# Both down-projections of a macaron decoder layer as seven half-size block products

## The chip, the cores and the metric

One core of a Trainium2 chip runs the whole layer as one program. The metric is the time of one execution on the device in microseconds (us), as the median of several runs. Engines that matter here: TensorE (PE) multiplies, VectorE (DVE) and ScalarE (ACT) prepare operands and take results away, GpSimd (POOL) does some element-wise work, and the queue of SyncE (SP) issues most transfers between DRAM and on-chip memory.

## What is computed

The layer has two feed-forward blocks, one at its start and one at its end, with attention between them. D = 1024 features, 1024 tokens, D_FF = 2816 hidden features:

```python
def swiglu(h, w1, w3, w2):
    return (jax.nn.silu(h @ w1) * (h @ w3)) @ w2

x = x + 0.5 * swiglu(rms_norm(x, norm_ffn1[l]), ffn1_w1[l], ffn1_w3[l], ffn1_w2[l])
...
x = x + 0.5 * swiglu(rms_norm(x, norm_ffn2[l]), ffn2_w1[l], ffn2_w3[l], ffn2_w2[l])
x = rms_norm(x, norm_out[l])
```

The change is in `(...) @ w2`, the product of the gated hidden values (called g here, 2816 x 1024 tokens) with w2 (2816 x 1024), and in how it is added to x.

## The kernel before

Everything is kept transposed: features on the 128 partitions, tokens along a row. A value of 32 bits is multiplied as two parts: `hi`, the rounded value in the type fp32r, and `lo`, what rounding took away. `split` (lines 162 and 163) makes them, `hi` by a copy on ACT and `lo` by a subtraction on DVE, or on POOL where a caller says so. `mm3` (lines 169 to 171) then does three matmuls, hi*hi, hi*lo and lo*hi, each 128 x 128 weights against up to 512 token columns.

**Up-projections.** `up` runs over eleven pairs c of 128-row hidden blocks (22 in all). For all pairs but the first, `strassen` already uses seven products in place of eight. The gated result of pair c, 128 x 2 x 1024 (j = 0, 1 are the two hidden blocks of the pair, then the tokens), is multiplied on POOL (line 493) and written to a DRAM tensor `ga`c in the first feed-forward and `gb`c in the second (line 494).

**Down-projections.** `down` goes through rounds, one for each half of the tokens h and half of the features fh (the second feed-forward takes its second half of the tokens as two pieces of 256 columns, all features at once). In a round it goes over the eleven pairs; each gives two k-blocks for four accumulators of 128 x 512 (PSUM tiles `mm` and `big`): 2 x 4 x 3 matmuls. The weights of the pair come by `unit` as one transfer of 512 KB into a `raw` tile (4 of them) on SP's queue, and are split into `w` and `v` tiles, `lo` on POOL in two of three cases. The g parts are read once per half of the tokens on ACT's queue (`load_g`, line 499) and kept in `a` tiles (33 in all) for both halves of the features. At a round's end DVE adds half of the accumulators to x (line 578). The rounds together are the plain eight block products of a 2 x 2 x 2 split, done at 1056 matmuls of 512 columns for the first feed-forward, and 528 of 512 and 1056 of 256 for the second.

**Order.** The program is written as one stream; a scheduler at build time moves instructions within it by priority and gives out tiles, and each engine then runs its own list strictly in order. Transfers wait in the issuing engine's list as any instruction does. `norm_x` (the next normalisation's scaling and squares) is stepped from inside the loop over `down`, and so are the output's statistics (`final_squares`, `final_stats`, `final_out`) in the second feed-forward.

Of the kernel before, what the change touches and what calls it, by code (L numbers as in the profile page):

```python
# [47 lines left out]
class Layer:  # L48
# [191 lines left out]
    def norm_x(self, gain, rt=None):  # L240


        self.r = self.a([P, 2, H])
        self.xn = [[], []]
        for h in range(2):
            acc = None
            for kp in range(4):
                x = self.x[h][kp]
                self.xn[h] += self.scaled(x, gain + 2 * kp)
                acc = self.squares([x], acc)  # L250
                if kp == 3:
                    self.late[h] = (acc, self.folded(acc), self.r[:, h], None if rt is None else rt[:, 4 * h:4 * h + 4])
                yield
# [216 lines left out]
    def up(self, base, name, ws, forms, beside=None):  # L470
# [4 lines left out]
        for c in range(1, NF // 2):  # L475
# [5 lines left out]
            for w in wv:  # L481
                for i, _ in enumerate(self.strassen(w)):
                    if c == NF // 2 - 1 and w is wv[1]:
                        if i == 1:
                            ready = [self.load_g(gd[n], 0) for n in range(2)]
                        if i == 5:
                            src = self.gated(gd, 0, ready)
                            self.g0 = src, [next(src)]
                outs.append(self.prod)
# [5 lines left out]
        return gd  # L495

    def load_g(self, d, h):
        raw = self.a([P, 2, H])
        self.nc.scalar.dma_start(out=raw, in_=d[:, :, h * H:h * H + H])
        return raw  # L500

    def gated(self, gd, h, ready=()):

        for c, d in enumerate(gd):
            raw = ready[c] if c < len(ready) else self.load_g(d, h)
            hi, lo = self.a([P, 2, H], F32R), self.a([P, 2, H], F32R)
            self.split(raw, hi, lo)
            yield hi, lo

    def down(self, base, gd, load, pieces=((0, 0, H), (1, 0, H))):  # L510
# [3 lines left out]
        g = {0: self.g0}  # L514

        def unit(c, fh, engine):
            raw = self.wr.tile([P, 2, H], F32, name="raw", tag="raw")
            u = base + U_W2A + 2 * c
            nc.sync.dma_start(out=raw, in_=self.wts[u:u + 2, :, fh * H:fh * H + H].rearrange("u p c -> p u c"))
            hi, lo = self.w([P, 2, H], F32R), self.v([P, 2, H], F32R)  # L520
            self.split(raw, hi, lo, engine)
            return hi, lo

        rounds = [(h, t0, t1, fh) for h, t0, t1 in pieces for fh in ((0, 1) if t1 - t0 == H else (None,))]
        for n, (h, t0, t1, fh) in enumerate(rounds):
            W = t1 - t0
            if fh is None:
                feats = list(range(8))
                ps = [self.big_ps([P, 2, 2, W]) for _ in range(2)] if n % 2 else [self.mm_ps([P, 2, W]) for _ in range(4)]
                ps = [p.rearrange("p a b t -> p (a b) t") for p in ps] if n % 2 else ps  # L530
                per = 4 if n % 2 else 2
            else:
                feats = list(range(4 * fh, 4 * fh + 4))
                ps = [self.big_ps() for _ in range(2)] if n % 2 else [self.mm_ps([P, 1, H]) for _ in range(4)]
                per = 2 if n % 2 else 1
            if n == 1:
                ahead = []
                g[1] = self.gated(gd, 1), ahead
            for kp in range(feats[0] // 2, feats[-1] // 2 + 1):
                if len(self.x[h]) <= kp:  # L540
                    self.x[h].append(load(h, kp))
            src, parts = g[h]
            for c in range(NF // 2):
                if len(parts) <= c:
                    parts.append(next(src))
                ws = []
                if fh is None:
                    ws += [self.weight(base + U_W2A + 2 * c + i, self.v if i else self.w, nc.vector if i else nc.gpsimd) for i in range(2)]
                else:
                    hi, lo = unit(c, fh, nc.vector if c % 3 == 2 else nc.gpsimd)  # L550
                    ws = [(hi[:, i], lo[:, i]) for i in range(2)]

                def one(i, f):
                    d = f - feats[0]
                    w = [v[:, d * P:d * P + P] for v in ws[i]]
                    self.mm3(ps[d // per][:, d % per], w, [v[:, i, t0:t1] for v in parts[c]],
                             c == 0 and i == 0 and d % per % 2 == 0 if W < H else c == 0 and i == 0,
                             c == NF // 2 - 1 and i == 1, W < H)

                if c == NF // 2 - 1:  # L560
                    for f in feats:
                        for i in range(2):
                            one(i, f)
# [649 lines left out]
    def run(self):  # L1213
# [14 lines left out]
        for step in self.down(0, gd, self.from_input):  # L1228
            if step is None:
                n += 1  # L1230
                if n in (2, 4, 6, 8, 9, 10):
                    next(norm)
# [130 lines left out]
```

## Time and profile before

| | |
|---|---|
| median of 3 runs | 2237.0 us (2234.97 to 2237.11) |
| the profiled execution | 2238.7 us, of which the span from first to last instruction is 2236.9 us |
| PE busy | 2187.7 us, 98% of the span |
| DVE / ACT / POOL busy | 56% / 44% / 26% |
| PE busy on the chain that ended last | 88% |
| data moved | 237.87 MB, 106 GB/s over the span |

The span falls into 40 slices on the page. The first down-projection lies between 494 and 737 us, the second between 1968 and 2223 us. Matmuls overlap in the records (each is shown for about twice its step), so what PE needs is read from the distance between two starts, not from the duration shown.

### The profile page before, as it was taken

How to read it: one execution, taken by the hardware profiler on the slowest of the kernel's cores; microseconds unless marked ns; L12 is line 12 of the kernel's file. 1: busy time of each engine (PE TensorE's matmuls, PEld its weight loads, DVE VectorE, ACT ScalarE, POOL GpSimd, SP SyncE). 2: the span in 40 equal slices, each digit the busy share in tenths (PEclk: the TensorE clock that was granted, in tenths of full speed). 3: DMA queues.
4: the chain of work that ended last, by engine and by line, in shares of the span. 5: the costliest groups of instructions: out<-in, count | busy, mean ns of one | idle time of the engine just before them, and what ended most of it. 6: DMA issues, size and time to landing. Idle time of an engine off the chain costs nothing.

```text
span 2236.9 us, 27311 instructions
## 1 busy us (share of the span) xinstructions
PE 2187.7 (98%) x10962; PEld 1849.2 (83%) x10962; DVE 1258.1 (56%) x1588; ACT 979.2 (44%) x1387; POOL 592.5 (26%) x363
## 2 busy tenths in 40 slices
PE   8999999999999999999999999999999999999997
PEld 7788888878888888878987788777888888878997
DVE  7964545443214677776556666867754545433433
ACT  6634333343323567654434354534433333433542
POOL 0033434353332000110011111100143434442353
PEclk9999999999999999999999999999999999999999
DMA  7322222256643211011123221222222222365654
GB/s 262 106 97 84 79 82 85 81 164 212 208 145 103 76 39 48 28 39 39 48 95 114 99 81 59 93 85 75 76 83 79 84 84 76 108 222 191 210 183 132
DMA packets 84639, 237.87 MB, mean 106 GB/s; under 512 B 7712, under 2 KB 10912, under 8 KB 84512
## 3 DMA queue, kind: packets, MB, share of 16 engines
q1 hardware_dynamic: 57328, 157.99, 22.2%
q0 software_dynamic: 15216, 55.06, 6.3%
q10 hardware_dynamic: 11968, 23.07, 3.2%
q8 instruction: 86, 1.41, 0.3%
q14 instruction: 41, 0.34, 0.0%
HBM read 191.00 MB, written 45.09 MB: 106 GB/s over the span
## 4 chain that ended last, share of the span: by engine, by line
PE 88%; DVE 6%; ACT 3%; issue 1%; DMA 1%; POOL 0%; SPq 0%; DVEq 0%; ACTq 0%; POOLq 0%
PE mm L170 17%; PE mm L169 17%; PE mm L171 17%; PE big L169 11%; PE big L170 11%; PE big L171 11%; PE big L896 1%; PE mm L942 1%; DVE a L163 1%; PE mm L218 1%; DMA raw<-in_wts_dram 1%; DVE w L163 1%; ACT t L147 1%; ACT w L162 1%; DVE v L163 0%
## 5 line engine op out<-in xcount | busy, mean ns | idle before, releaser
L169 PE MATMUL mm<-a,w 128*128 128x512 f32 (+1 forms) x1536 | 588.2, 383 | 5.6 <-ACT w L162 5.5
L170 PE MATMUL mm<-a,w 128*128 128x512 f32 (+1 forms) x1536 | 585.5, 381 | 5.0 <-DVE a L163 5.0
L162 ACT CAST w<-raw 128x1024 fp32r<-128x1024 f32 (+1 forms) x315 | 310.5, 993 | 503.4 <-PE mm L170 213.5
L163 POOL TENSOR_TENSOR v<-raw,w 128x1024 fp32r<-128x1024 f32 x120 | 290.3, 2419 | 621.2 <-ACT w L162 617.2
L171 PE MATMUL mm<-a,v 128*128 128x512 f32 (+1 forms) x1056 | 401.6, 380 | 0.0
L169 PE MATMUL big<-a,w 128*128 128x512 f32 (+1 forms) x1024 | 391.8, 383 | 5.3 <-DVE a L789 4.3
L170 PE MATMUL big<-a,w 128*128 128x512 f32 (+1 forms) x1024 | 390.2, 381 | 0.9 <-DVE a L163 0.8
L169 PEld LDWEIGHTS mm<-a,w 128*128 128x128 f32 x1536 | 291.8, 190 | 60.4 <-ACT w L162 5.5
L170 PEld LDWEIGHTS mm<-a,w 128*128 128x128 f32 x1536 | 291.7, 190 | 60.0 <-DVE a L163 7.2
L171 PE MATMUL big<-a,v 128*128 128x512 f32 (+1 forms) x800 | 302.9, 379 | 0.0
L171 PE MATMUL mm<-a,w 128*128 128x512 f32 (+1 forms) x632 | 233.4, 369 | 0.5 <-DVE w L163 0.5
L171 PEld LDWEIGHTS mm<-a,v 128*128 128x128 f32 x1056 | 198.6, 188 | 37.6
L169 PEld LDWEIGHTS big<-a,w 128*128 128x128 f32 x1024 | 193.0, 188 | 43.2 <-ACT a L783 4.5
L170 PEld LDWEIGHTS big<-a,w 128*128 128x128 f32 x1024 | 193.0, 188 | 37.8 <-DVE a L163 1.7
L163 DVE TENSOR_TENSOR a<-a 128x1024 fp32r<-128x1024 f32 (+2 forms) x105 | 126.0, 1210 | 160.1 <-ACT a L162 159.9
L417 DVE TENSOR_TENSOR a<-a,mm 128x1024 f32<-128x1024 f32 x40 | 48.9, 1221 | 258.6 <-PE mm L171 258.6
L171 PEld LDWEIGHTS big<-a,v 128*128 128x128 f32 x800 | 151.0, 189 | 28.6 <-issue 0.7
L163 DVE TENSOR_TENSOR w<-raw,w 128x1024 fp32r<-128x1024 f32 (+1 forms) x107 | 150.0, 1404 | 35.9 <-PE big L170 20.3
L162 ACT CAST a<-a 128x1024 fp32r<-128x1024 f32 (+2 forms) x105 | 98.2, 945 | 154.2 <-DMA a<-gb 61.0
L171 PE MATMUL big<-a,w 128*128 128x512 f32 (+1 forms) x440 | 162.6, 370 | 0.0
L171 PEld LDWEIGHTS mm<-a,w 128*128 128x128 f32 x632 | 121.7, 193 | 20.2 <-DVE w L163 1.0
L163 DVE TENSOR_TENSOR v<-raw,w 128x1024 fp32r<-128x1024 f32 x66 | 83.7, 1271 | 59.5 <-ACT w L162 59.2
(208 smaller groups left out, 3173.5 us busy)
## 6 DMA issues: line engine op xcount, KB each, us to landing
raw<-in_wts_dram SPq DMA_DIRECT2D x265, 512.0 KB, 3.7
ga<-a POOLq DMA_DIRECT2D x22, 512.0 KB, 2.9
a<-ga ACTq DMA_DIRECT2D x22, 512.0 KB, 4.4
gb<-a POOLq DMA_DIRECT2D x22, 512.0 KB, 2.9
a<-gb ACTq DMA_DIRECT2D x22, 512.0 KB, 4.6
a<-in_x_dram SPq DMA_DIRECT2D x16, 512.0 KB, 6.2
xm<-a POOLq DMA_DIRECT2D x8, 512.0 KB, 5.2
a<-xm POOLq DMA_DIRECT2D x8, 512.0 KB, 10.0
```

Of the source, the lines that this page charges most:

```text
L147: ins = self.nc.scalar.activation(out, in_, func, **kw)
L162: copy = self.nc.scalar.copy(hi, full)
L163: (engine or self.nc.vector).tensor_tensor(lo, full, hi.bitcast(F32), op=ALU.subtract)
L169: mm(ps, w[0], x[0], start=start, stop=False, skip_group_check=more)
L170: mm(ps, w[0], x[1], start=False, stop=False, skip_group_check=more)
L171: mm(ps, w[1], x[0], start=False, stop=stop, skip_group_check=more)
L218: self.nc.tensor.matmul(ps, self.ones_r if m is None else m, v, start=i == 0, stop=i == len(parts) - 1)
L417: nc.vector.tensor_tensor(out[1], c, b1.unsqueeze(1).broadcast_to([P, 2, H]), op=ALU.add)
L896: nc.tensor.matmul(ps[:, c, :n], qs[m][:, i, iq], xs[c][:, m, :n], start=i == 0, stop=i == 1)
L942: nc.tensor.matmul(op[:, ib % 4 * P:ib % 4 * P + P], v[jb // 4][:, jb % 4, par], at[:, jb * P:jb * P + P], start=jb == 0, stop=jb == ib)
```

## The change

The token halves h, the feature halves fh and the two blocks j of each pair make g and w2 into 2 x 2 blocks: G(j,h) with 1408 rows in eleven blocks of 128, W(j,fh) likewise. `down` now takes Strassen's scheme in Winograd's form: seven products, in the order 1, 5, 6, 3, 7, 4, 2, each over all eleven hidden blocks (five steps of two blocks and a last one of one) with four accumulators of 128 x 512. The operands are sums and differences of blocks, made on DVE (`less`, line 521 of the new file) from blocks that are read again for each product:

- product 1: G(0,0) with W(0,0); product 2: G(1,0) with W(1,0); product 3: G(1,1) with a sum of four W blocks; product 4: a sum of four G blocks with W(1,1); products 5, 6, 7: sums of two or three blocks on both sides.
- Products 6 and 7 go on in the accumulators of product 1, and product 3 in those of product 5. The accumulators are added to x after each product, to one quarter of x, after product 7 to two.
- g and w2 are read as transfers of 256 KB, two for a `raw` tile, all on SP's queue. Both splits are on ACT and DVE; POOL has no splits there any more. Running sums are kept in six `a` tiles (g) and six `v` tiles (weights). The g operands are made six steps ahead of PE, the weights' two.
- In the second feed-forward only product 2 is taken in two pieces of 256 columns. `final_squares` takes the other two feature pairs first, and the second half of the tokens is finished first.
- `norm_x` runs over the second half of the tokens first, and the first `diff_proj` after it does both of its projections for that half before the other.

```diff
-    def norm_x(self, gain, rt=None):
+    def norm_x(self, gain, rt=None, order=tuple((h, kp) for h in range(2) for kp in range(4))):
...
+        for h, kp in order:
+            x = self.x[h][kp]
+            self.xn[h][2 * kp:2 * kp + 2] = self.scaled(x, gain + 2 * kp)
...
                 for i, _ in enumerate(self.strassen(w)):
-                    if c == NF // 2 - 1 and w is wv[1]:
-                        if i == 1:
-                            ready = [self.load_g(gd[n], 0) for n in range(2)]
-                        if i == 5:
-                            src = self.gated(gd, 0, ready)
-                            self.g0 = src, [next(src)]
+                    if i == 1 and w is wv[1] and c == NF // 2 - 1:
+                        down = self.down(base, gd, load, pieces)
+                        with self.tc.high_priority(60):
+                            next(down)
...
+        order = (1, 5, 6, 3, 7, 4, 2)
+        pairs = [list(range(c, min(c + 2, NF // 2))) for c in range(0, NF // 2, 2)]
...
+        def read_g(i, j, h, t=None):
+            t = t or self.wr.tile([P, 2, H], F32, name="raw", tag="raw")
+            for m, c in enumerate(pairs[i]):
+                nc.sync.dma_start(out=t[:, m], in_=gd[c][:, j, h * H:h * H + H])
+            return t
...
+        def make_g(n, i):
+            if n == 1:
+                full = sums_g[i] = read_g(i, 0, 0, self.a([P, 2, H]))
+            elif n in (5, 6, 4):
+                raw = read_g(i, *{5: (0, 1), 6: (1, 1), 4: (1, 0)}[n])
+                full = sums_g[i]
+                less(i, full, raw, full)
+            else:
+                full = read_g(i, *{3: (1, 1), 7: (0, 0), 2: (1, 0)}[n])
+                if n == 7:
+                    less(i, full, sums_g[i], full)
+            forms_g[n, i] = parts(i, full, self.a([P, 2, H], F32R), self.a([P, 2, H], F32R))
+
+        def make_w(n, i):
+            last = n == order[-1]
+            if n == 5:
+                full = sums_w[i] = read_w(i, 0, 1, self.v([P, 2, H]))
+                less(i, full, full, read_w(i, 1, 1), ALU.add)
+            elif n == 6:
+                full = sums_w[i]
+                less(i, full, full, read_w(i, 0, 0))
+            else:
+                full = read_w(i, *{1: (0, 0), 3: (1, 0), 7: (1, 1), 4: (1, 1), 2: (1, 0)}[n])
+                if n in (3, 7):
+                    less(i, full, full, sums_w[i])
+            forms_w[n, i] = parts(i, full, self.w([P, 2, H], F32R), (self.v if last else self.w)([P, 2, H], F32R))
...
+        def add(ps, h, fh, t0=0, t1=H):
+            for kp in range(2):
+                xs = x_of(h, 2 * fh + kp)
+                for d in range(2):
+                    nc.vector.scalar_tensor_tensor(xs[:, d, t0:t1], ps[2 * kp + d], 0.5, xs[:, d, t0:t1],
+                                                   op0=ALU.mult, op1=ALU.add)
...
+        ahead_g, ahead_w = n_pairs, 2
...
+            steps = [(m, d) for m in range(len(pairs[i])) for d in range(4)]
+            for m, d in sorted(steps, key=lambda v: v[::-1]) if end else steps:
+                one(m, d)
+            if end:
+                for h, fh in {1: [(0, 0)], 5: [(1, 1)], 6: [(1, 0)], 3: [(1, 0)], 7: [(0, 1), (1, 1)], 4: [(0, 1)],
+                              2: [(0, 0)]}[n]:
+                    add(ps, h, fh, t0, t1)
...
-        pieces = ((0, 0, H), (1, 0, M), (1, M, H))
+        pieces = ((0, M), (M, H))
```

Where the instructions stand. On SP, at the end of the first up-projection, before: the weights of the first rounds, one transfer of 128 x 2 x 512 for each `raw`.

```order
L370 DMA raw_3323<-in_wts_dram 128x1024
L519 DMA raw_3563<-in_wts_dram 128x2x512
L519 DMA raw_3597<-in_wts_dram 128x2x512
L519 DMA raw_3633<-in_wts_dram 128x2x512
L519 DMA raw_3669<-in_wts_dram 128x2x512
```

After, late in product 3 of the first down-projection (`ga`n are the blocks of g, `in_wts_dram` the weights):

```order
L516 DMA raw_4405<-in_wts_dram 128x512 x2
L510 DMA raw_4437<-ga6_732 128x512
L510 DMA raw_4437<-ga7_733 128x512
L516 DMA raw_4445<-in_wts_dram 128x512
L510 DMA raw_4476<-ga8_734 128x512
L510 DMA raw_4476<-ga9_735 128x512
L516 DMA raw_4484<-in_wts_dram 128x512 x2
```

Blocks of g have joined the weights in the four `raw` tiles and on SP's list, in pieces of half the size.

On DVE, in the middle of the first down-projection, before: the last splits of g (`a<-a`), one of weights (`v<-raw,w`), and additions to x at a round's end (line 578) beside the next normalisation (line 198).

```order
L163 TENSOR_TENSOR a_4348<-a_4345,a_4347 128x1024
L163 TENSOR_TENSOR v_4424<-raw_4421,w_4423 128x1024
L163 TENSOR_TENSOR a_4664<-a_4661,a_4663 128x1024
L578 SCALAR_TENSOR_TENSOR a_3957<-big_3955,a_3957 128x1024
L198 SCALAR_TENSOR_TENSOR a_4769<-a_3559,gains_85,a_4768 128x512
L578 SCALAR_TENSOR_TENSOR a_3959<-big_3956,a_3959 128x1024
```

After, at the end of product 3 (line 521 makes a sum, line 163 a `lo` part; the last row is the weights' `lo` for the first step of product 7, made from `raw_4484`):

```order
L521 TENSOR_TENSOR raw_4437<-a_3568,raw_4437 128x1024
L521 TENSOR_TENSOR raw_4445<-raw_4445,v_3985 128x512
L163 TENSOR_TENSOR w_4410<-raw_4405,w_4409 128x1024
L163 TENSOR_TENSOR a_4442<-raw_4437,a_4441 128x1024
L521 TENSOR_TENSOR raw_4476<-a_3575,raw_4476 128x1024
L521 TENSOR_TENSOR raw_4484<-raw_4484,v_3773 128x1024
L163 TENSOR_TENSOR w_4449<-raw_4445,w_4448 128x512
L163 TENSOR_TENSOR a_4481<-raw_4476,a_4480 128x1024
L521 TENSOR_TENSOR raw_4516<-a_3582,raw_4516 128x512
L163 TENSOR_TENSOR a_4520<-raw_4516,a_4519 128x512
L521 TENSOR_TENSOR raw_4523<-raw_4523,v_3815 128x1024
L163 TENSOR_TENSOR w_4489<-raw_4484,w_4488 128x1024
```

Sums and splits now alternate there, and a `raw` tile that holds a sum (4437, 4476, 4484) stays in use from its sum to its split.

## Rows read from the trace of the kernel before

**Rows 1.** Page, busy time, share of the span and instructions of three engines.

```profile
PE 2187.7 (98%) x10962; PEld 1849.2 (83%) x10962; DVE 1258.1 (56%) x1588; ACT 979.2 (44%) x1387; POOL 592.5 (26%) x363
```

**Rows 2.** Page, granted TensorE clock in 40 slices, in tenths (9: 90% or more).

```profile
PEclk9999999999999999999999999999999999999999
```

**Rows 3.** Busy time by stretch: both down-projections (columns: stretch, length, engines, clock, DMA).

```profile
core 0: us, PE busy (x) PEld busy (x) DVE busy (x) ACT busy (x) POOL busy (x), PEclk, DMA share, GB/s
494.20:736.00 241.80, 239.32 (x1054) 197.48 (x1053) 77.42 (x65) 79.78 (x83) 79.08 (x40) 1.00 0.51 165
1975.00:2222.00 247.00, 245.87 (x1573) 223.73 (x1572) 89.85 (x70) 100.75 (x112) 104.09 (x44) 1.00 0.58 190
```

**Rows 4.** Timeline of PE: 60 matmuls of 512 columns apart, 58 of 256 columns.

```profile
470.39 0.39 PE L169 MATMUL mm<-a,w 128*128 128x512 f32 x1
...
484.00 0.39 PE L169 MATMUL mm<-a,w 128*128 128x512 f32 x1
...
2211.36 0.28 PE L169 MATMUL big<-a,w 128*128 128x256 f32 x1
...
2218.32 0.28 PE L170 MATMUL big<-a,w 128*128 128x256 f32 x1
```

**Rows 5.** Timeline of PE: first matmuls of the first down-projection, of the mixer; second down-projection.

```profile
494.19 0.61 PE L169 MATMUL mm<-a,w 128*128 128x512 f32 x2
496.16 0.50 PE L170 MATMUL mm<-a,w 128*128 128x512 f32 x1 [1.35 <-DVE a L163]
...
736.71 0.39 PE L169 MATMUL mm<-a,w 128*128 128x512 f32 x1
...
1969.82 0.50 PE L170 MATMUL mm<-a,w 128*128 128x512 f32 x1 [1.35 <-DVE a L163]
1976.50 0.50 PE L170 MATMUL mm<-a,w 128*128 128x512 f32 x1 [1.13 <-DVE a L163]
```

**Rows 6.** Timeline of DVE in the first up-projection: instructions back to back.

```profile
99.38 1.23 DVE L332 TENSOR_TENSOR a<-a 128x1024 f32<-128x1024 f32 x1
100.52 0.69 DVE L453 TENSOR_TENSOR a<-big,t 128x512 f32<-128x512 f32 x1
...
107.11 0.68 DVE L463 TENSOR_TENSOR a<-mm,a 128x512 f32<-128x512 f32 x1
107.71 1.22 DVE L332 TENSOR_TENSOR a<-a 128x1024 f32<-128x1024 f32 x1
```

**Rows 7.** Timelines of DVE and POOL at the head of the first down-projection.

```profile
499.37 3.42 DVE L163 TENSOR_TENSOR a<-a 128x1024 fp32r<-128x1024 f32 x1
...
499.28 2.42 POOL L493 TENSOR_TENSOR a<-a 128x1024 f32<-128x1024 f32 x1
```

**Rows 8.** Groups by shape, 494.2 to 736.7 us (busy us, mean ns, idle before).

```profile
L162 ACT CAST w<-raw 128x1024 fp32r<-128x1024 f32 x42 | 44.1, 1051 | 97.3 <-PE mm L170 41.8 <-PE big L170 32.3 <-issue 9.7
L163 DVE TENSOR_TENSOR a<-a 128x1024 fp32r<-128x1024 f32 x22 | 32.0, 1456 | 75.9 <-ACT a L162 75.9
L198 DVE SCALAR_TENSOR_TENSOR a<-a,gains 128x512 fp32r<-128x512 f32 x13 | 11.7, 932 | 5.5 <-PE big L170 3.4 <-ACT a L197 2.0
L212 DVE TENSOR_TENSOR a<-a 128x1024 f32<-128x1024 f32 x4 | 7.7, 1922 | 2.0 <-ACT a L208 2.0
```

**Rows 9.** SP's issues and landing: line 519 (512 KB loads), then the output (256 KB).

```profile
L519 SPq DMA_DIRECT2D raw<-in_wts_dram x66: 367/368/384, 444.9 to 2041.6; - x66
...
DMA to landing us min/median/max: 3.4/3.7/7.1
...
out_dram<-a SPq DMA_DIRECT2D x4, 256.0 KB, 2.1
```

**Rows 10.** Transfers from 494.2 to 736.7 us, and in the kernel's last 7 us.

```profile
DMA packets 18892, 40.01 MB, mean 165 GB/s; under 512 B 1216, under 2 KB 1216, under 8 KB 18880
...
a<-ga ACTq DMA_DIRECT2D x20, 512.0 KB, 4.3
...
GB/s 0 0 0 0 0 0 0 0 0 0 0 0 0 0 0 0 0 29 322 386 380 340 141 363 392 380 258 322 392 386 351 170 380 398 386 217 0 0 0 0
```

More of the change, by code (lines that the diff above doesn't have):

```diff
@@ L238, in stats @@
             self.rstd(ps, D, rt)
-    def norm_x(self, gain, rt=None):
+    def norm_x(self, gain, rt=None, order=tuple((h, kp) for h in range(2) for kp in range(4))):
         self.r = self.a([P, 2, H])
[L244 to L253, printed above, removed]
+        self.xn = [[None] * NK, [None] * NK]
+        accs, left = [None, None], [4, 4]
+        for h, kp in order:
+            x = self.x[h][kp]
+            self.xn[h][2 * kp:2 * kp + 2] = self.scaled(x, gain + 2 * kp)
+            accs[h] = acc = self.squares([x], accs[h])
+            left[h] -= 1
+            if left[h] == 0:
+                self.late[h] = (acc, self.folded(acc), self.r[:, h], None if rt is None else rt[:, 4 * h:4 * h + 4])
+            yield
     def normed(self, steps, gain, rt=None):
@@ L468, in first_pair, with up @@
             pass
-    def up(self, base, name, ws, forms, beside=None):
+    def up(self, base, name, load, pieces, ws, forms, beside=None):
         nc = self.nc
@@ L494, in up @@
                 nc.gpsimd.dma_start(out=gd[c][:, j].rearrange("p (h t) -> p h t", h=2), in_=g)
[L495 to L508, printed above, removed]
@@ L510, in down @@
-    def down(self, base, gd, load, pieces=((0, 0, H), (1, 0, H))):
-        nc = self.nc
[L514 to L521, printed above, removed]
-            return hi, lo
-        rounds = [(h, t0, t1, fh) for h, t0, t1 in pieces for fh in ((0, 1) if t1 - t0 == H else (None,))]
-        for n, (h, t0, t1, fh) in enumerate(rounds):
-            W = t1 - t0
[L527 to L548, printed above, removed]
-                else:
[L550 to L563, printed above, removed]
-                else:
-                    for i in range(2):
-                        for f in feats:
-                            one(i, f)
-                if n == 1 and c > 0:
-                    ahead.append(next(g[1][0]))
-                if n == len(rounds) - 1 and c < NF // 2 - 1:
-                    yield None
-            for kp in range(feats[0] // 2, feats[-1] // 2 + 1):
-                x = self.x[h][kp][:, :, t0:t1]
-                for d in range(2 * kp - feats[0], 2 * kp - feats[0] + 2, min(per, 2)):
-                    m = min(per, 2)
-                    p = ps[d // per][:, d % per:d % per + m]
-                    xs = x[:, d % 2:d % 2 + m]
-                    nc.vector.scalar_tensor_tensor(xs, p, 0.5, xs, op0=ALU.mult, op1=ALU.add)
-                yield h, kp
@@ L1222, in from_spill @@
             return x
-        self.x = [[], []]
+        self.x = [[None] * 4, [None] * 4]
         self.rt = self.sp.tile([P, 8], F32, name="rt", tag="rt")
-        norm = self.norm_x(G_MIX, self.rt)
-        n = 0
[L1228 to L1232, printed above, removed]
-            elif step[0] and step[1] >= 2:
+        norm = self.norm_x(G_MIX, self.rt, [(1, kp) for kp in range(4)] + [(0, kp) for kp in (2, 3, 0, 1)])
+        for s, _ in enumerate(down):
+            if 30 <= s < 34 or 36 <= s < 38 or s == 41:
                 next(norm)
+        for _ in norm:
+            pass
         self.spare = nc.vector
@@ L1237, in run @@
         forms, ws = self.cross()
-        gd = self.up(U_F2, "b", ws, forms)
-        self.x = [[], []]
-        pieces = ((0, 0, H), (1, 0, M), (1, M, H))
-        down = self.down(U_F2, gd, from_spill, pieces)
+        pieces = ((0, M), (M, H))
+        down = self.up(U_F2, "b", from_spill, pieces, ws, forms)
+        self.x = [[None] * 4, [None] * 4]
         def go(n):
```

100 lines of the change are left out of this document (84 added, 16 removed).

## Prediction

> **What bounds the kernel now.** I read the page's busy times first, then the clock, then the timelines of both down-projections. PE is busy 98% of the span and no other engine over 56% [rows 1], at a granted clock of 2.4 GHz, the upper of its two levels, in every slice [rows 2]. In the two stages that change, PE is busy 239.3 of 241.8 and 245.9 of 247.0 us, while DVE, ACT and POOL each stay under 43% [rows 3]. So the stage ends when PE has done its matmuls, and a matmul taken off PE is worth its step, as long as the other engines deliver. The step: 60 matmuls of 512 columns start within 484.00 - 470.39 = 13.61 us, 0.2268 us each; 58 of 256 columns within 6.96 us, 0.1200 us each [rows 4], which is more than half of 0.2268. What PE loses in the first stage is at its head: the stage lasts 736.71 - 494.19 = 242.5 us [rows 5], its 1056 matmuls need 1056 x 0.2268 = 239.5, so 3.0 us are lost, where the first `lo` parts of g come late. The second stage has waits of 1.35 and 1.13 us in the same place [rows 5].
>
> **Matmuls, on the path.** Seven products of 11 blocks x 4 accumulators x 3 matmuls are 924 for each down-projection. First stage: 1056 - 924 = 132 of 512 columns go, 132 x 0.2268 = 29.9 us. Second stage: before, 528 x 0.2268 + 1056 x 0.1200 = 246.5 us; after, six products are 792 of 512 columns and product 2 is 264 of 256 columns, 179.6 + 31.7 = 211.3 us; 35.2 us go, of which 30 are the eighth product and 5 the halves that are no longer used. Together **65.1 us**. The instruction lists agree (792 rows of 256 columns fewer, 132 of 512 more). Nothing else changes on PE but order.
>
> **DVE, beside PE.** This is what pays. For each stage there are 77 splits of 128 x 1024 (7 products x 5.5 steps x 2 sides), all on DVE now, and 44 sums of that size (22 on g, 22 on weights), 121 instructions; plus 36 additions to x of 128 x 512 from PSUM. Back to back, a 128 x 1024 instruction costs 100.52 - 99.38 = 1.14 us, a 128 x 512 one from PSUM 107.71 - 107.11 = 0.60 us [rows 6]. That is 137.9 + 21.6 us, and at most 26 for `norm_x` (16 x 0.93 + 6 x 1.92, prices of [rows 8]): 186 of the 209.6 us that PE now needs, 89%. ACT does 77 copies of 1.05 us [rows 8], 81 us, and is no bound. It isn't even, though: PE takes 29.9 us for a product, and DVE has 22 instructions (25.1 us) and 4 additions (2.4) during products 5 and 3, 17 + 4 during 6, 22 + 8 (29.9 us) during 7, and little during 1, 4 and 2. The weights are made two steps (10.9 us) ahead, so DVE's list may lag by some us before PE notices.
>
> The price rests on POOL's silence. At the head of the stage a DVE subtraction took 3.42 us beside a POOL multiplication of 2.42 us, and the mean of the 22 in the stage is 1.456 us [rows 7, 8]. The two multiplications of the last hidden pair are still there afterwards; POOL's splits are not, so I take 1.14. The Trainium skill ("SBUF - State Buffer", section "SBUF: two separate sides") says that DVE with two SBUF inputs and GpSimd share a port pair as a lock, and that the loser waits for the whole instruction. By that page the sum is the one above; at the stage's mean, 121 x 1.456 + 21.6 + 26 = 224 us, DVE would set the stage and 14 us of each gain would go.
>
> **Transfers and the four `raw` tiles.** After, a stage reads 77 pieces of g and 88 of weights of 256 KB, and x: 181 x 0.262 = 47 MB in some 212 us, 224 GB/s, against 165 before [rows 3, 10]; the queue moves up to 398 GB/s [rows 10]. What matters is how soon a `raw` tile is filled again, since DVE's list is fixed: SP issues two transfers (0.37 us each, so the second 0.42 later) and a 512 KB load lands 3.7 us after issue in the median, 3.4 to 7.1; stores of 256 KB landed in 2.1 [rows 9], reads of g in 4.3 [rows 10]. A 256 KB load is in no row. The turn is thus between 0.42 + 2.1 = 2.5 and 0.42 + 7.1 = 7.5 us; I take 0.42 + 3.7 = 4.1, nearest to the median loads, and up to 5.3 under the heavier traffic.
>
> I walked DVE's list through product 3, with PE's end of product 1 as zero (products 5, 6 and 3 follow). Product 6 ends at 59.8; the additions that wait for it and the splits behind them follow. Up to the sum in `raw_4405` DVE runs at its own pace, to 72.7. `raw_4437` takes the tile that a split at 69.3 frees: with a turn of 4.1 its sum ends at 74.5, `raw_4484` (freed at 76.2) at 81.5, `raw_4523` (freed at 82.0) at 87.3, and the `lo` part of product 7's first weights at 88.4. PE wants it at 89.9. No loss, 1.5 us in hand. With 5.3 the same walk gives 92.1 for it and 99.7 for the second step's: losses of 2.2 and 2.1. With 7.5 it is 15 us in these places and, by the same pattern of sum, copy and split in product 7, some 7 more. Products 5 and 6 have six DVE instructions (6.8 us) between a tile's release and its next use and lose nothing below that. I take **2 us** a stage, 4 in all, from bounds of 0 and 22 a stage.
>
> The Trainium skill ("DMA: Bandwidth & Descriptors", "Anatomy of one DMA" and "Bandwidth") speaks against halves: each transfer pays about 2.0 us beside its bytes at 436 GB/s, and one should batch to 1 MiB. An estimate from that page is 2.6 us for 256 KB, a turn of 3.0, no loss in the walk; only if transfers did not overlap would 181 of them take over 400 us. No row shows a 256 KB load alone.
>
> **Heads, ends, and what is moved.** At the head the g blocks now come through SP behind weight reads into `v` tiles that the last `strassen` still holds; step 1's g is issued at about 491.5 and its `lo` done near 498.5 to 500, wanted at 499.8 and slowed by POOL's two multiplications. Bounds 0 and 4.5 us lost, 2 taken where 3.0 was lost: a gain of 1 a stage, **2 in all**. The mixer's first two projections start on the half that is final early, 48 matmuls (10.9 us) over product 2's additions (4 x 0.6) and their scaling; that covers it, and the start at 736.71 shows no wait today either. In the second stage the first output stores wait on SP for POOL, ahead of the last two weight loads; I estimate 16.3 us into product 4 for the statistics' place on PE, some 8 for sums and root, 4 x 2.42 on POOL [rows 7]: stores out near 34, the loads' `lo` near 41, wanted at 45; free, up to 5 us if late. The tail (addition, square, four sums on PE, root, output) keeps its form: 0.
>
> **The sum.** -65.1 + 4 - 2 = -63.1. On the profiled execution, 2238.7, that is 2175.6; the median of the runs, 2237.0, lies 1.7 lower and gives **2174 us**, 2.8% faster. The stages would last about 212 and 219 us.
>
> **Rivals.**
> - *The `raw` tiles set the pace.* With turns of 6 to 7 us in the dense products, both stages lose 10 to 22 us. For it: four tiles, three DVE instructions between release and use in product 3, 36% more traffic. Against: 3.7 us loads now. Time: 2237 - 67 + 20 to 44, **2190 to 2214**.
> - *DVE pays the contended price and becomes the bound; slower.* Place: every sum and split. A stage is as long as before when 121p + 21.6 + 26 = 242.5, p = 1.61 us; at 2.58 us, between a free and a blocked instruction [rows 6, 7], a stage takes 360 us and the kernel about **2470**. For it: a mean of 1.456 now with POOL a third busy. Against: POOL is nearly empty after.
> - *All is covered.* Heads vanish and no product waits: 2237 - 65 - 6, **2166 to 2170**.
> - *It does not do what it says*: PE gets no shorter because a granted clock falls to 1.2 GHz in the stages after pauses. No slice shows that now [rows 2]; it would cost more than it gives.
>
> **Chances.** Forecast (2170 to 2184) 0.56, all covered 0.14, `raw` tiles (2184 to 2214) 0.24, DVE bound or clock, 2220 and above, 0.06. About 0.2%, 4.5 us, is what a measurement of this kernel tells from no change. Faster by more 0.95, within 0.02, slower 0.03. The range, 2166 to 2200, leaves out the upper part of the second rival and the last: some 0.17.
>
> **What would show it.** 10,300 PE instructions; PE at a step of 0.227 in the products; DVE at 85 to 90% and POOL near nothing in the stages; `L163 DVE` at 1.2 us. Waits of PE for line 163 at the change from product 3 to 7 show the `raw` tiles, waits spread evenly over the products DVE's price. Wrong if PE waits over 10 us in a stage, or if DVE's mean is over 1.4 us.

## The result and the profile after

The changed kernel takes **2178.1 us** (median of 4 runs, 2176.6 to 2179.4) against 2236.7 for the kernel before in the same session. The ratio is 0.974, with a 95% interval of 0.972 to 0.976: 58.6 us less. The prediction was 2174, with a range of 2166 to 2200. The profiled execution took 2177.1 us (span 2175.3); against the profiled one of before it is 61.6 shorter, of which 2.5 arise in the first 65 us of the program, which the change doesn't touch (last section).

The page's busy times, to be read against [rows 1]:

```profile
PE 2123.4 (98%) x10302; PEld 1777.6 (82%) x10302; DVE 1432.4 (66%) x1810; ACT 980.4 (45%) x1401; POOL 417.7 (19%) x293
```

PE lost 660 instructions and 64.3 us of busy time, and is still busy 98% of the span: it bounds the kernel as before. DVE gained 174 us, POOL lost 175. By stretch, for both down-projections (columns as in [rows 3]):

```profile
core 0: us, PE busy (x) PEld busy (x) DVE busy (x) ACT busy (x) POOL busy (x), PEclk, DMA share, GB/s
491.70:705.70 214.00, 210.96 (x925) 173.12 (x924) 173.75 (x180) 93.35 (x104) 8.23 (x11) 1.00 0.70 227
1939.70:2161.60 221.90, 217.94 (x1069) 182.62 (x1068) 169.75 (x173) 94.05 (x112) 22.15 (x12) 1.00 0.63 204
```

From its first matmul to the first of the mixer, the first stage went from 242.5 to 214.0 us (28.5 less). From its first matmul to the start of its last, the second went from 254.6 to 222.3 (32.3 less), and the tail behind it got 1.1 shorter (14.5 to 13.4). DVE is now busy 81% of the first stage, and the transfers take 70% of the DMA engines' time. Against these gains, the part between the stages got 2.9 us longer (1231.1 to 1234.0). That arises at the mixer's start: by its 200th matmul PE is 3.7 us later than before, and the attention behind it, which the change doesn't touch, gives 0.8 back. What PE still waits for, in the first stage and the mixer's start, and then in the second stage and the tail (us in total, times, longest):

```profile
PE mm L218 <- ACT v L162: 1.6, 2, 1.4
PE mm L170 <- DVE a L163: 1.5, 2, 0.8
PE big L171 <- DVE w L163: 1.0, 1, 1.0
PE mm L169 <- ACT a L162: 0.5, 1, 0.5
...
PE mm L1314 <- DVE a L212: 1.5, 1, 1.5
PE mm L170 <- DVE a L163: 1.5, 2, 0.8
PE big L171 <- DVE w L163: 1.5, 1, 1.5
PE mm L171 <- DVE v L163: 0.8, 1, 0.8
PE mm L169 <- ACT a L162: 0.2, 1, 0.2
```

`mm L170` and `mm L169` are the heads of the stages, `big L171` is inside product 5, `mm L171 <- DVE v` is in product 2, L218 is the mixer's start and L1314 the tail. No wait at the change from product 3 to 7 is in the list.

**Inside product 5.** These are the rows of DVE around the end of product 1, and the matmul of PE that waited:

```profile
526.03 2.96 DVE L163 TENSOR_TENSOR a<-a 128x1024 fp32r<-128x1024 f32 x3
528.90 2.48 DVE L563 SCALAR_TENSOR_TENSOR a<-mm,a 128x512 f32<-128x512 f32 x4
...
535.83 1.22 DVE L163 TENSOR_TENSOR w<-v,w 128x1024 fp32r<-128x1024 f32 x1
...
537.11 0.50 PE L171 MATMUL big<-a,w 128*128 128x512 f32 x1 [1.05 <-DVE w L163]
```

PE had finished product 1 by about 524.5. DVE reached its additions to x (L563) 4.4 us later, since it was still splitting g for product 5, and the `lo` part of product 5's third weights came at 537.05, just too late. DVE was not full in product 1, though: of its 32.8 us it was busy 24.0. The longest of its pauses there stands behind a copy on ACT that waited for a block of g:

```profile
508.66 1.05 ACT L162 CAST a<-a 128x1024 fp32r<-128x1024 f32 x1 [3.96 <-DMA a<-ga]
...
509.74 1.23 DVE L163 TENSOR_TENSOR a<-a 128x1024 fp32r<-128x1024 f32 x1 [3.68 <-ACT a L162]
```

So the backlog comes from blocks of g that land late as well as from the work. No run moves these transfers.

**At the mixer's start.** PE's rows, before and after (L218 sums the squares of q and k; before, the first four sums stood behind the whole second projection, the next four 48 matmuls later, and neither waited):

```profile
761.30 1.09 PE L218 MATMUL mm<-v,bd_r 128*128 128x512 f32 x4
```

```profile
730.07 0.39 PE L171 MATMUL mm<-a,w 128*128 128x512 f32 x1
731.88 0.96 PE L218 MATMUL mm<-v,bd_r 128*128 128x512 f32 x3 [1.43 <-ACT v L162]
733.07 2.13 PE L218 MATMUL mm<-v,bd_r 128*128 128x512 f32 x5 [0.22 <-ACT v L162]
735.00 0.41 PE L169 MATMUL mm<-w,a 128*128 128x256 f32 x1
...
736.92 0.29 PE L169 MATMUL mm<-w,a 128*128 128x256 f32 x1
```

PE pauses 1.43 us for the squares of q. From 735.00 to 736.92 nine matmuls of 256 columns take 0.213 us each where they take 0.12 otherwise: the granted clock there is 0.50, the 1.2 GHz level. The same stretch by windows, at a mean clock of 0.74:

```profile
730.46:737.00 6.54, 4.90 (x18) 3.99 (x19) 4.65 (x7) 4.51 (x7) 0.00 (x0) 0.74 0.25 80
```

### The profile page after: what moved, and what is told of

It reads as the page before. It is cut to its first block, busy times and chain, and to the rows that moved or that the text cites. A ratio compares the mean times of both kernels' runs of the same rounds, so it can differ in the third digit from the quotient of the medians.

```text
span 2175.3 us, 26505 instructions
## 1 busy us (share of the span) xinstructions
PE 2123.4 (98%) x10302; PEld 1777.6 (82%) x10302; DVE 1432.4 (66%) x1810; ACT 980.4 (45%) x1401; POOL 417.7 (19%) x293
## 5 line engine op out<-in xcount | busy, mean ns | idle before, releaser
L169 PE MATMUL mm<-a,w 128*128 128x512 f32 (+1 forms) x1580 | 605.1, 383 | 6.7 <-ACT w L162 5.9
L170 PE MATMUL mm<-a,w 128*128 128x512 f32 (+1 forms) x1580 | 602.1, 381 | 3.1 <-DVE a L163 3.0
L169 PE MATMUL big<-a,w 128*128 128x512 f32 x936 | 366.9, 392 | 5.1 <-DVE a L824 4.3
L170 PE MATMUL big<-a,w 128*128 128x512 f32 x936 | 365.3, 390 | 0.9 <-DVE a L163 0.8
L169 PEld LDWEIGHTS mm<-a,w 128*128 128x128 f32 x1580 | 299.1, 189 | 64.1 <-ACT w L162 6.1
L170 PEld LDWEIGHTS mm<-a,w 128*128 128x128 f32 x1580 | 298.9, 189 | 59.6 <-DVE a L163 4.9
L171 PE MATMUL mm<-a,v 128*128 128x512 f32 (+1 forms) x836 | 316.1, 378 | 0.8 <-DVE v L163 0.8
L171 PE MATMUL mm<-a,w 128*128 128x512 f32 (+1 forms) x808 | 310.5, 384 | 0.5 <-DVE w L163 0.5
L163 POOL TENSOR_TENSOR v<-raw,w 128x1024 fp32r<-128x1024 f32 x72 | 174.0, 2417 | 402.7 <-ACT w L162 402.7
L171 PE MATMUL big<-a,w 128*128 128x512 f32 x616 | 240.8, 391 | 2.5 <-DVE w L163 2.5
L163 DVE TENSOR_TENSOR w<-raw,w 128x1024 fp32r<-128x1024 f32 (+1 forms) x155 | 206.2, 1332 | 31.6 <-ACT w L162 14.4
L169 PEld LDWEIGHTS big<-a,w 128*128 128x128 f32 x936 | 176.1, 188 | 42.8 <-ACT a L818 4.5
L417 DVE TENSOR_TENSOR a<-a,mm 128x1024 f32<-128x1024 f32 x40 | 48.8, 1221 | 244.5 <-PE mm L171 244.5
L170 PEld LDWEIGHTS big<-a,w 128*128 128x128 f32 x936 | 176.2, 188 | 37.8 <-DVE a L163 1.6
L171 PEld LDWEIGHTS mm<-a,v 128*128 128x128 f32 x836 | 157.3, 188 | 30.2 <-DVE v L163 1.0
L171 PEld LDWEIGHTS mm<-a,w 128*128 128x128 f32 x808 | 153.6, 190 | 30.4 <-DVE w L163 1.0
L171 PE MATMUL big<-a,v 128*128 128x512 f32 x448 | 175.2, 391 | 0.0
L171 PEld LDWEIGHTS big<-a,w 128*128 128x128 f32 x616 | 116.1, 188 | 28.4 <-DVE w L163 4.2
L163 DVE TENSOR_TENSOR a<-a 128x1024 fp32r<-128x1024 f32 (+2 forms) x109 | 116.5, 1082 | 32.3 <-ACT a L162 32.1
L491 POOL TENSOR_TENSOR a<-a 128x1024 f32<-128x1024 f32 x40 | 96.4, 2409 | 48.1 <-DVE a L417 45.9
```

What stands on the lines that cost most here:

```text
L163: (engine or self.nc.vector).tensor_tensor(lo, full, hi.bitcast(F32), op=ALU.subtract)
L169: mm(ps, w[0], x[0], start=start, stop=False, skip_group_check=more)
L170: mm(ps, w[0], x[1], start=False, stop=False, skip_group_check=more)
L171: mm(ps, w[1], x[0], start=False, stop=stop, skip_group_check=more)
L417: nc.vector.tensor_tensor(out[1], c, b1.unsqueeze(1).broadcast_to([P, 2, H]), op=ALU.add)
L491: nc.gpsimd.tensor_tensor(g, g, u, op=ALU.mult)
```

## The experiments

The theory that the two traces gave: PE sets both stages; each is worth the matmuls taken off it, less a loss of 3 to 4 us; that loss is at the heads and in DVE's backlog at the end of product 1, not in the `raw` tiles; some 3 us go at the mixer's start. Its rivals: the `raw` tiles set the pace, or DVE does, for its own length or for POOL's port. "Before" stood at 2236.6 to 2236.8 us in all three sessions. Stage lengths below are of PE and measured as above.

### One stage at a time

e_only1 runs the changed first stage and mixer start with the old second down-projection; e_only2 is the kernel before with the new second down-projection alone.

```
e_only1:  gd = self.up_old(U_F2, "b", ws, forms); down = self.down_old(U_F2, gd, from_spill, pieces)
e_only2:  gd = self.up_old(0, "a", *self.mem_kv()); for step in self.down_old(0, gd, self.from_input): ...
```

> The changed first stage with its mixer start; the second down-projection is that of the kernel before. By the prediction's sum the first stage is worth 29.9 - 2 + 1 = 28.9 us: 2208. By the changed kernel's profile (stage shorter by 28.5, mixer's start longer by 3 to 3.5): 25 us, about 2211.5. If the two gains depend on each other (the rival to adding them): this run and its counterpart with only the second stage changed do not add up to the 58.6 us of the whole, by more than 2 us.

> The kernel before up to the cross-attention; only the second down-projection is changed. Prediction's sum: 35.2 - 2 + 1 = 34.2 us, 2203. By the changed kernel's profile: 33 for the stage and 0.5 at the end, 2203.5. With the run that changes only the first stage it should add up to 58.6 us within 2.

Measured: 2210.7 us (ratio 0.9885, interval 0.987 to 0.990) and 2202.5 (0.985, 0.9835 to 0.9865): 25.9 and 34.1 us less, 60.0 together against 58.6 for the whole. The gains add up within what was allowed. The second stage's run comes to what the prediction's terms for it say, 34.2, but in its trace the stage is only 32.3 us shorter and the tail 1.1, for which nothing was written. The first falls 3 short of its 28.9: in its trace the stage is 28.4 us shorter and the part up to the second stage 2.0 longer, at the mixer's start.

### More work for DVE

```
+            hi, lo = forms_w[n, i]
+            nc.vector.tensor_tensor(lo[:, 0], full[:, 0], hi[:, 0].bitcast(F32), op=ALU.subtract)
```

> The changed kernel, with one more subtraction of 128x512 for each weight block of a step on VectorE (the first half of its lo part is made twice): 42 a stage, 0.6 to 0.7 us each, 25 to 29 us of VectorE a stage. Theory (TensorE sets the stage, VectorE has slack that is uneven: none in product 5, some in products 6 to 2): 5 to 8 us a stage slower than the changed kernel, 10 to 16 in all, in product 5 above all: 2188 to 2194. Rival, slack everywhere: under 2 us, 2178 to 2180. Rival, VectorE already sets the pace: 25 a stage, about 2230.

Measured: 2192.3 us (0.9805, 0.979 to 0.982), 14 more than the changed kernel. The first stage grew by 5.2 us and the second by 10.0, out of some 25 added to DVE in each. So DVE has room, but not everywhere: the longest waits are the old ones of product 5, grown (2.79 us in the first stage, 2.77 in the second), and a new one in the second stage's product 2, two steps ahead of the old:

```profile
543.15 0.79 PE L171 MATMUL big<-a,w 128*128 128x512 f32 x1 [2.79 <-DVE w L554]
...
2149.83 0.39 PE L171 MATMUL mm<-a,v 128*128 128x256 f32 x1 [3.21 <-DVE v L554]
```

Not all of the growth is waiting. Behind each of these three waits the granted clock fell to 0.50 for some 3.5 us, which is, as an estimate, 1.7 us of lost matmul time each, 5 of the 15.

### Three raw tiles

```
-        self.wr = ctx.enter_context(tc.tile_pool(name="wr", bufs=4))
+        self.wr = ctx.enter_context(tc.tile_pool(name="wr", bufs=3))
```

> The changed kernel with three raw tiles in place of four. Two raw tiles are used a step of 5 us, so a tile's cycle may last 10 us with four and 7.5 with three; the turn is 4.6 us (0.42 and 4.2), and a sum or a copy and a split hold a tile 1.2 to 2.5 us more. Theory (with four there is some room, with three none): 3 to 15 us a stage, in products 3 and 7 and not in 4 and 2; 2184 to 2208. Rival, the raw tiles set the pace with four already: the products lengthen by up to a third where they are used twice a step, 20 us a stage and more, 2220 and up. Rival, they don't matter: under 2 us.

Measured: 2213.8 us (0.990, 0.988 to 0.992), 36 more, above the theory's range. The pool serves the whole program, and some 7 us are lost before the first stage begins, which the expectation had left out. The first stage takes 227.3 us, 13 more, and the second is 17 longer. In the first stage DVE's rows show how, and PE's where (at the end of product 3 and in product 7):

```profile
610.34 1.23 DVE L521 TENSOR_TENSOR raw<-a,raw 128x1024 f32<-128x1024 f32 x1 [1.63 <-DMA raw<-ga]
...
612.75 0.50 PE L171 MATMUL big<-a,w 128*128 128x512 f32 x1 [2.02 <-DVE w L163]
...
645.67 0.79 PE L171 MATMUL mm<-a,w 128*128 128x512 f32 x1 [3.97 <-DVE w L163]
```

With four tiles the same stretch of DVE has stalls of 0.3 to 0.9 us for transfers, and PE no wait at this change of product. In the second stage the expectation was wrong on the place too: the longest wait, 5.59 us, is in product 2, which it had left out. There seven weight loads stand behind the output stores on SP (three with four tiles), and PE waits for the first of them:

```profile
2163.76 7.33 SPq L516 DMA_DIRECT2D raw<-in_wts_dram  x7
...
2169.53 0.58 PE L169 MATMUL mm<-a,w 128*128 128x256 f32 x1 [5.59 <-ACT w L162]
```

The prediction's rival on the `raw` tiles is thus the right mechanism one tile further down: four tiles suffice, three don't. Five were not tried.

### Larger transfers

```
-            for m, c in enumerate(pairs[i]):
-                nc.sync.dma_start(out=t[:, m], in_=self.wts[base + U_W2A + 2 * c + j, :, fh * H:fh * H + H])
+            src = self.wts[u:u + 2 * n].rearrange("(m j) p f -> p j m f", j=2)
+            nc.sync.dma_start(out=t[:, :n], in_=src[:, j, :, fh * H:fh * H + H])
```

> The changed kernel with a step's two weight reads of 256 KB issued as one of 512 KB. Theory (with four raw tiles there are some 5 us in hand at the tightest place, so a shorter turn buys nothing): 2176 to 2179, within 1 us; a 512 KB read lands 3.4 to 4.5 us after its issue, no later than the second of two halves now (0.42 + 4.1). By the Trainium skill (DMA: Bandwidth & Descriptors, on batching) fewer and larger transfers should help; as a rival this would be a gain of 2 us or more. Rival on the other side (a tile filled in one piece comes later because two halves use more of the queue's engines at once): 1 to 4 us slower.

Measured: 2177.1 us (0.974, 0.973 to 0.975), the same as the changed kernel. The weights' rows among the transfers of the first stage (KB each, median us to landing), changed kernel and experiment:

```profile
raw<-in_wts_dram SPq DMA_DIRECT2D x69, 256.0 KB, 4.1
```

```profile
raw<-in_wts_dram SPq DMA_DIRECT2D x37, 512.0 KB, 4.5
```

A tile of two halves is full 0.42 + 4.1 = 4.5 us after its first issue, and a tile of one piece after 4.5: nothing is won. The Trainium skill (DMA: Bandwidth & Descriptors, "Anatomy of one DMA") gives a fit for transfers that GpSimd issues: a fixed 2.0 us and the bytes at 436 GB/s. As an estimate from that page it makes 2.6 us for 256 KB and 3.2 for 512. These loads are issued by SP, beside other transfers (227 GB/s in the stage), and show longer times for both and a smaller gap between them.

### POOL back at work

The `lo` parts of the weights go to POOL in two pair steps of three, as the kernel before shared them.

```
-            self.split(*(v[:, :len(pairs[i])] for v in (full, hi, lo)))
+            self.split(*(v[:, :len(pairs[i])] for v in (full, hi, lo)), engine)    # weights: nc.vector if i % 3 == 2 else nc.gpsimd
```

> The changed kernel with the lo parts of the weights on GpSimd for two pair steps of three, 28 of a stage's 42, as the kernel before shared them. VectorE sheds 28 x 1.14 = 32 us a stage. If VectorE's price rises only to the 1.456 us of the kernel before, its sum stays the same (93 x 1.456 + 21.6 + 26 = 183 against 186) and the stage too: 2178 to 2183. If a GpSimd instruction holds VectorE off for its whole 2.42 us, the two engines' times add up to 154 + 68 = 222 us in a stage of 212: 10 us and more a stage, 2198 to 2220. If GpSimd costs VectorE nothing, the waits of product 5 go: 2175.

Measured: 2242.5 us (1.0026, 1.0017 to 1.0035), **66 more than the changed kernel: the whole gain is gone**, far beyond all that was expected. The first stage lasts 245.8 us, longer than before the change. Windows of the two stages, and groups of the first (busy us, mean ns):

```profile
491.50:720.00 228.50, 206.62 (x849) 164.48 (x848) 175.13 (x149) 88.86 (x100) 81.25 (x36) 0.94 0.64 201
1971.00:2220.00 249.00, 224.45 (x1003) 182.65 (x1002) 167.79 (x144) 92.21 (x111) 88.39 (x34) 0.94 0.56 178
...
L163 DVE TENSOR_TENSOR a<-raw,a 128x1024 fp32r<-128x1024 f32 x15 | 28.5, 1897 | 15.0 <-ACT a L162 15.0
...
L521 DVE TENSOR_TENSOR v<-v,raw 128x1024 f32<-128x1024 f32 x10 | 18.7, 1870 | 0.0
...
L163 POOL TENSOR_TENSOR w<-v,w 128x1024 fp32r<-128x1024 f32 x8 | 26.7, 3339 | 47.4 <-ACT w L162 36.9 <-DMA raw<-in_wts_dram 10.5
```

The same DVE groups take 1221 and 1219 ns in the changed kernel. DVE does fewer instructions and is busy as long, and POOL's own price reaches 3.3 us, against 2.4 for its multiplications in the changed kernel: either engine's instructions get longer beside the other's. The Trainium skill (SBUF — State Buffer, "SBUF: two separate sides") tells of a shared port pair that is held for a whole instruction; these rows agree. And it doesn't stop there. A late weight makes PE pause, and behind each pause of 2.8 us and more in these stages the granted clock fell to 0.50:

```profile
550.79 0.80 PE L171 MATMUL big<-a,w 128*128 128x512 f32 x1 [3.56 <-POOL w L163]
551.39 0.63 PE L169 MATMUL big<-a,w 128*128 128x512 f32 x1
551.81 0.63 PE L170 MATMUL big<-a,w 128*128 128x512 f32 x1
552.24 0.63 PE L171 MATMUL big<-a,w 128*128 128x512 f32 x1
```

Matmuls of 512 columns start 0.43 us apart here, where the step is 0.227 elsewhere. By the windows' mean clock of 0.94 this is, as an estimate, 14 of the 32 us by which the first stage grew (0.06 x 228.5), and PE's longer waits are most of the rest.

### Who is late in product 5, and at the mixer's start

Four runs, and the changed kernel again beside them. e_same has no edit. e_wfirst writes a step's weights ahead of its g:

```
             while done_w < ...: make_w(*total[done_w])      # was behind the loop on g
             while done_g < ...: make_g(*total[done_g])
```

e_defer moves product 1's additions to x; their accumulators are next written by product 6:

```
+            if n == 5 and i == 4:
+                add(sets[1], 0, 0)
-            if end:
+            if end and n != 1:
```

e_mixer puts the square sums of q and k behind the projection that follows (both `later` entries are made after q's last half, and the empty step behind them goes); e_both has the edits of e_defer and e_mixer.

> The changed kernel again, unchanged, as the base for the three runs beside it: 2178 (2176.6 to 2179.4 so far). In its profile the granted clock at the mixer's start either falls to 0.50 behind the 1.4 us pause, as it did in the changed kernel's profile, or stays at 1.00, as in two of the experiments with the same pause.

> The changed kernel with the weight forms of a step written ahead of its g forms; nothing else. Theory (the loss inside the products is VectorE's lag at the end of product 1, where the forms of g for product 5 stand ahead of the weights for product 5): the waits at product 5's third step (1.05 us in the first stage, 1.50 in the second) go, 2 to 2.5 us faster than the unchanged one: 2175.5 to 2176. Rival (VectorE is full in product 5, so the wait only changes place): within 1 us of it. Rival (weights first makes the g forms late at the head): slower by 1 to 3.

> The changed kernel with product 1's four additions to x (2.48 us of VectorE) moved from behind product 1 to behind product 5's fifth step; their accumulators are next written by product 6. Theory (TensorE's wait of 1.05 to 1.51 us at product 5's third step is VectorE's backlog, in which these additions stand ahead of the weights): that wait goes in both stages and none as long takes its place, since product 6 leaves VectorE room: 1 to 3 us faster than the changed kernel, 2174 to 2176. Rival (VectorE has no room in product 5 either, the wait reappears one to three steps later): within 0.7 us of it, 2176 to 2178.

> The changed kernel, but at the mixer's start the square sums of q and k stand behind the next projection (48 matmuls of 256 columns) in place of directly behind the last of q's. Theory (the pause of 1.43 us at 730.07 is the chain of ACT and VectorE behind the late root of half 0, and the low granted clock behind it follows from the pause): pause and low clock both go, 1.65 us plus about 1.7 where the clock fell: 2174.7 to 2176.5. Rival (the low clock has another cause): 1.65 us alone and the clock still falls there in the profile. Rival (the later square sums delay the first attention head by as much): no change.

> The deferred additions together with the later square sums at the mixer's start. If the two losses are separate, their gains add up: 1 to 3 and 2.75 us, 2171 to 2173.5. If only the mixer's part is real: 2174.

| | us | range | ratio to before | first stage, us |
|---|---|---|---|---|
| e_same | 2176.9 | 2174.8 to 2181.8 | 0.974 (0.972 to 0.975) | 214.2 |
| e_wfirst | 2183.0 | 2180.2 to 2185.9 | 0.976 (0.9745 to 0.977) | 215.2 |
| e_defer | 2173.7 | 2171.2 to 2175.0 | 0.972 (0.970 to 0.973) | 212.6 |
| e_mixer | 2174.1 | 2173.1 to 2175.1 | 0.972 (0.9705 to 0.973) | 214.7 |
| e_both | 2176.5 | 2172.3 to 2177.9 | 0.973 (0.972 to 0.974) | 214.9 |

*e_defer* agrees with the theory in the first stage. The split of product 5's third weights now ends at 535.1 instead of 537.1, and the wait there is gone in both stages. In the first stage this is worth 1.6 us. In the second it is worth 0.4, since a wait in product 7 takes most of its place:

```profile
2066.05 0.50 PE L171 MATMUL mm<-a,w 128*128 128x512 f32 x1 [1.33 <-DVE w L163]
```

*e_wfirst* was a miss for all three expectations. The waits of product 5 do go, but the stages get longer, the second by 4.6 us. DVE's and POOL's rows in product 4 show why:

```profile
2128.68 10.10 DVE L163 TENSOR_TENSOR v<-raw,w 128x1024 fp32r<-128x1024 f32 x3
...
2125.81 11.88 POOL L1329 TENSOR_TENSOR a<-a,t 128x1024 f32<-128x1024 f32 x4 [176.60 <-DVE t L185]
```

Three splits of product 2's weights run beside POOL's four multiplications for the output, at 3.4 us each. In e_same splits meet POOL there as well, but they begin 4.5 us earlier, reckoned from the stage's first wait; and on SP four weight loads now stand behind the output stores, where it was three. Product 2 waits five times for its weights, 3.4 us in all, and behind the last of these waits the granted clock is 0.51 for 3.4 us. The second stage's head waits 1.1 us more for g as well, as the last rival said. The order's cost was set mostly in a place that it was not changed for.

*e_mixer*: the pause is gone; after the projection's last matmul at 730.53 the next starts at 730.76, and the clock stays at 1.00.

```profile
730.53 0.39 PE L171 MATMUL mm<-a,w 128*128 128x512 f32 x1
730.76 0.28 PE L169 MATMUL mm<-w,a 128*128 128x256 f32 x1
```

2.8 us by the medians. In the profiles of e_same and e_mixer 2.5 us are won at the mixer's start, and about 0.8 of it is lost again at the first attention head, so the last rival holds in part. In e_same's profile the clock did not fall behind the pause, so these 1.7 us hold nothing for a fall; the rest of the 2.8 is within the ranges of the runs.

*e_both* missed: by the medians the two gains do not add up. Its trace shows where the time went. The mixer's start is as fast as in e_mixer, and the second stage takes 220.1 us against e_same's 222.7. Against this, the first stage has a wait of 1.84 us in product 7 and is no shorter. Then there is a wait of 1.77 us for a first weight at 56.6 us, which is no part of either edit. And in the attention the granted clock falls behind a pause of 1.58 us that e_mixer has too, without a fall, at 933.46 (rows of e_both):

```profile
935.88 0.96 PE L948 MATMUL big<-a 128*128 128x512 f32 x4 [1.58 <-DVE s L951]
...
938.44 0.63 PE L171 MATMUL mm<-a,w 128*128 128x512 f32 x1
```

This fall costs about 1.6 us, in a part that neither edit touches. Whether the gains add up is thus not shown either way, with ranges of 2 to 7 us in each of these kernels. e_defer alone is about 3 us faster than the changed kernel, of which its stages explain 2.0; that is at the edge of what such runs can tell.

## Why the prediction was right, and where its steps were off

**Matmuls, -65.1:** right. PE's instructions fell to 10,302, its busy time by 64.3 us; stage by stage 28.5 and 32.3 us went where 28.9 and 34.2 net were written down. The run with the second stage alone gave 34.1, with the tail's 1.1 in it, where the prediction had 0: PE's wait there fell from 2.27 to 1.52 us.

**DVE's price, 1.14:** right, and it is what the gain hangs on. The group `v<-v,raw` shows 1219 ns for an instruction, with starts 1.14 apart. DVE's 186 us became 174, and its 85 to 90% became 81, because `norm_x` was taken at its contended prices and wholly inside the stage, and because the first stage has 32 additions to x, not 36. The mechanism of the rival on DVE's price is real: with POOL at work e_pool's five largest groups of DVE cost 112.2 us for 68 instructions, 1.65 each, and the first stage came out as long as before. That the rival put its turning point at 1.61 is a coincidence: it reckoned with 121 instructions on DVE, e_pool has 93, and DVE is idle for a quarter of that stage. What made the stage long there was late weights and the low clock behind them.

**The raw tiles:** no loss at the change from product 3 to 7, as the walk said with a turn of 4.1. The turn measured 0.42 + 4.1 to 4.3, or about 4.6, a little above the value taken. The walk had the `lo` part of product 7's first weights at 88.4 and wanted at 89.9. Reckoned from the end of product 1 (524.57) it was done at 87.7 and wanted at about 91.8:

```profile
611.07 1.22 DVE L163 TENSOR_TENSOR w<-raw,w 128x1024 fp32r<-128x1024 f32 x1
```

The estimate from the Trainium skill's page, a turn of 3.0, was too low.

**The 2 us inside the products: right in size by luck, wrong in place.** They were taken for the `raw` tiles; the waits were 1.05 us (product 5), 1.50 (product 5) and 0.76 (product 2), and none of them stands at the change from product 3 to 7. The step that failed is "little during 1, 4 and 2". In product 1 DVE makes all forms of g for product 5, weights of product 1 and the first of product 5: 20 instructions of line 163 and 521, 24 us of work with one of the up-projection, in which it also waited for late g, and it ended 4.4 us late. In product 4 it was busy for 27.4 of 29.9 us. The walk began at the end of product 1 as zero, with DVE on time, and so could not see this; "Products 5 and 6 ... lose nothing" held for the `raw` tiles that it spoke of, not for DVE's list. e_defer shows that the backlog makes the wait: 2.4 us less ahead of those weights, and it is gone.

**Heads, 2 taken:** measured 0.77 + 0.46 + 0.76 = 2.0 in the first stage, 1.7 in the second.

**The mixer's start, 0: the term that was wrong,** by 2.9 us up to the second stage (3.7 at the place itself). "48 matmuls (10.9 us) over product 2's additions and their scaling; that covers it" looked at x alone. The half that is final late also owns a root mean square, whose chain is statistics on PE (723.44), then ACT and DVE up to 728.3; only then can k's and q's last halves be scaled and squared. Before, k's four sums stood behind the whole of q's projection (761.30 us) and q's four behind the 48 matmuls after that (767.98); now k's last half has one projection behind it and q's none, and both are of the late half. e_mixer, which puts 48 matmuls between, takes the pause away. This term accounts for most of the 4 us by which 2174 fell short; the second stage's 1.9 and the tail's 1.1 partly cancel.

**Output stores ahead of the weight loads, 0 (up to 5):** nearly right in what it cost, 5 us off in time. These are SP's rows in the second stage and the matmul that waited:

```profile
2123.87 9.45 SPq L1333 DMA_DIRECT2D out_dram<-a  x4
2133.41 1.67 SPq L516 DMA_DIRECT2D raw<-in_wts_dram  x3
...
2140.36 0.39 PE L171 MATMUL mm<-a,v 128*128 128x256 f32 x1 [0.76 <-DVE v L163]
```

Three loads stood behind the stores, not two. The stores were out 39 us into product 4, not 34, the weights' `lo` was done at 46, not 41, and that was 0.76 us after it was wanted: the 4 us in hand were used up.

## What to carry to other kernels

Taking matmuls off a kernel that PE bounds is worth their step, if what has to be made for the fewer products fits beside them on one engine: here sharing that work between DVE and POOL cost more than the matmuls saved, and DVE alone did not. Count a helper engine's list by when it must be done, with the backlog that the previous stage leaves, and not by when its results are used. When the order of halves is turned round, follow everything that hangs on the half that is now last (its statistics, and the sums behind them), not only the data.

## What the runs showed of the hardware

- The same pause of PE, 1.43 us at the mixer's start, was followed by a granted clock of 0.50 in three profiles (the changed kernel's, e_extra's and e_pool's) and by 1.00 throughout in six (e_only1, e_raw3, e_same, e_wfirst, e_defer, e_batch). e_same's rows beside those above:

```profile
732.17 0.96 PE L218 MATMUL mm<-v,bd_r 128*128 128x512 f32 x3 [1.43 <-ACT v L162]
733.35 1.43 PE L218 MATMUL mm<-v,bd_r 128*128 128x512 f32 x5 [0.22 <-ACT v L162]
734.86 0.39 PE L169 MATMUL mm<-w,a 128*128 128x256 f32 x1
735.09 0.28 PE L170 MATMUL mm<-w,a 128*128 128x256 f32 x1
```

  From 733.07 to the tenth matmul at 736.92 it is 3.85 us with the fall; the same matmuls take 2.7 without it. So waits of 1.65 us can cost 2.8, and one profile doesn't tell which. The pause of 1.58 us in the attention is in all thirteen profiles and was followed by such a fall in three (e_raw3, e_both, e_batch).
- The program's first 65 us come in two lengths, whatever the kernel: one matmul that waits for the same split starts at 61.8 to 62.5 us in seven profiles (the changed kernel's among them) and at 64.3 to 64.7 in four (that of before among them). In the first, 16 or 17 matmuls of 256 columns start between 15 and 17 us, in the second 9 or 10. (The other two, e_raw3 and e_both, have a further wait there.) The clock's row shows 1.00 there in both kinds, so what sets it is open. It is 2.5 of the 3.0 us by which the profiled saving exceeds the medians'.
